# A hybrid RG-LRU and attention trunk: new order of products, operand work and sums in the feed-forward units, and overlapped chains at their ends

## The chip, the core and the metric

The kernel runs on one core of a Trainium2 chip. The metric is the device time of one execution in microseconds. A core has these engines, each with a queue that it works off in order: TensorE (PE in the profile; PEld is its loading of stationary operands), VectorE (DVE), ScalarE (ACT), GpSimd (POOL) and SyncE (SP), which here only starts transfers. Semaphores order the work between engines. Matmuls read SBUF and write PSUM, of which there are eight banks of 512 float32 columns in each of 128 partitions.

## The reference

`x` is one sequence of 512 tokens with 1024 features, in float32. Layer 0 mixes tokens by an RG-LRU, layer 1 by stick-breaking attention with 16 heads; each is followed by a feed-forward block of 2816 hidden features, which the change is about.

```python
D_MODEL, SEQ, DEPTH, D_FF = 1024, 512, 2, 2816

def _rmsnorm(x, g):
    y = x * lax.rsqrt(jnp.mean(x * x, axis=-1, keepdims=True) + RMS_EPS)
    return y * g

def _swiglu(h, w_gate, w_up, w_down):
    g = h @ w_gate
    u = h @ w_up
    return (jax.nn.silu(g) * u) @ w_down

for i in range(DEPTH):
    x = x + mixer_i(_rmsnorm(x, norm_mix_g[i]))     # RG-LRU, then attention
    x = x + _swiglu(_rmsnorm(x, norm_ffn_g[i]), ffn_w_gate[i], ffn_w_up[i], ffn_w_down[i])
return _rmsnorm(x, final_g)
```

## The kernel before

Every float32 factor is split into a high and a low part, and a product is the sum of three matmuls (`mm3`): high by high, high by low, low by high. So each chunk of weights, 128 x 1024 float32, has to be loaded and split before use: ScalarE casts `wh` (L294), and VectorE, or for a few chunks POOL, subtracts to get `wl` (L295).

The feed-forward block uses a Strassen-like scheme with seven products in place of eight, written g1 to g7 for the gate and up matrices and d1 to d7 for the down matrix. Some products take sums of weight blocks. For gate and up, these sums are mostly made by DMA: POOL starts transfers that add a block to a buffer in SBUF (`Piece.plus`, L87 to 90). The buffers are `bu` (g5, then g6, then g4, one after the other in the same place), `bv` (g3, g7) and `raw` (g1, g2). For the down matrix POOL makes them by four subtractions for each unit (`DownPiece.after`, L150 to 159, listed as L152). In units 0, 1 and 5 VectorE adds one sum directly (`direct`, L54 and L113).

The hidden features are worked in units 0 to 5 (`NU` = 5): 512 columns of weights in units 0 to 4, with two chunks a product, and 256 in unit 5, with one chunk. Unit u has its own g products and, from unit 1 on, the d products on the hidden features of unit u-1. Two more chunks ("last") follow. At the end of the g products of a unit come silu and the gating; the result is turned by PE transposes (t0 and t1, L697) and made into the operands ha, hb and ht on ScalarE and VectorE (`operands`, L699 to 710). PSUM: two pairs of banks, A and B, for the g products; `db` and `tb` for the d products, with `tb` also for the turns.

The order is written by hand. In `ffn` all four compute engines keep program order, and there are two orders as strings: one for the chunks in `Unit` (L54 to 62), one for the steps in `ffn` (L841 to 848). `chunk()` (L317) takes the next chunk, splits chunks up to 4 ahead of it, and starts loads up to 9 ahead (`more`). What `soon` (L258) was given is issued when the next chunk is taken. `hold` (L247, L666) bounds how far the first unit is loaded while the stage before still runs.

Unit 0 has two steps of its own: the turn of the residual stream into y (x0 to x3, `turned`), and `stats` (L818), the norm's scale, which PE computes by summing `acc` (L465). Behind layer 0's block, PE multiplies the last two chunks, turns y back (`back`, L861) and makes the normalised input of attention (`norm_in`, L388), where V's products come first (L336 to 338). Behind layer 1's block `finish` (L476 to 494) adds the last products, does the final norm in four blocks of 128 tokens, one after the other, and stores.

Of the kernel before, what the change touches and what calls it, by code (L numbers as in the profile page):

```python
# [16 lines left out]
P = 128  # L17
S = 512
# [26 lines left out]
class Unit:  # L45
    def __init__(self, kern, l, u):
# [22 lines left out]
class Piece:  # L69
    LOADS = {1: ("raw", 0), 2: ("raw", 2), 5: ("bu", 0), 3: ("bv", 3)}  # L70
    HOME = {1: 1, 2: 2, 5: 5, 6: 5, 4: 5, 3: 3, 7: 3}
    NEXT = {5: 3, 6: 2, 3: 1}
    last = {}

    def __init__(self, unit, q, c):
        self.unit, self.q, self.c = unit, q, c
        self.pool = (q, c) in ((7, 1), (2, 1)) and unit.u > 0 and unit.np == 2

# [13 lines left out]
    def ready(self):  # L92
        old = self.last.get((self.unit.kern, self.c))
        return self.q != 5 or old is None or old.u == self.unit.u or (old, 4, self.c) in self.unit.kern.done

    def load(self):
# [6 lines left out]
        if q == 5:  # L103
            self.plus(1)
            self.last[kern, self.c] = un
# [4 lines left out]
    def sums(self):  # L110
        un, kern = self.unit, self.unit.kern
        if self.q == 6 and un.direct:
# [17 lines left out]
class DownPiece(Piece):  # L130
    def __init__(self, unit, q):
        self.unit, self.q, self.c = unit, q, 0
        self.pool = q in (5, 4)

    def ready(self):
        return True

    def load(self):
        un, kern = self.unit, self.unit.kern
        for k in {1: ("11",), 2: ("21",), 6: ("12", "22")}.get(self.q, ()):  # L140
            t = un.d[k] = kern.raw_buf() if self.q < 6 else self.buf("d" + k, kern.fp, 1)
            kern.nc.sync.dma_start(t, un.down[("11", "21", "12", "22").index(k)])

    def source(self):
        return self.unit.d[{1: "11", 2: "21", 6: "t", 5: "11", 7: "12", 3: "22", 4: "t"}[self.q]]

    def sums(self):
        pass

    def after(self):  # L150
        kern, d = self.unit.kern, self.unit.d
        sub = lambda o, x, y: kern.soon(lambda: kern.nc.gpsimd.tensor_tensor(d[o], d[x], d[y], ALU.subtract))  # L152
        if self.q == 1:
            d["t"] = self.buf("dt", kern.fp, 1)
            sub("11", "12", "11")
            sub("t", "22", "11")
            sub("12", "22", "12")
        elif self.q == 6:
            sub("t", "21", "t")


class Kern:
    def __init__(self, ctx, tc, a, out):
# [15 lines left out]
        self.later, self.done = deque(), set()  # L179
# [40 lines left out]
    def plan(self):  # L220
# [26 lines left out]
        self.hold = next(i for i, e in enumerate(full) if isinstance(e, Piece)) + 6  # L247
# [10 lines left out]
    def soon(self, f):  # L258
        self.later.append((self.used, f))
# [57 lines left out]
    def chunk(self, ahead=None):  # L317
# [3 lines left out]
        while self.later and self.later[0][0] <= i:  # L321
# [954 lines left out]
```

## Time and profile before

| what | us |
|---|---|
| three executions | 1199.16, 1203.34, 1203.98 (median 1203.34) |
| the profiled execution | 1200.12, its span 1198.4 |
| RG-LRU layer | from 0 to 167.6 |
| feed-forward block 0 | from 167.6 to about 545 |
| attention | from about 545 to 815.8 |
| feed-forward block 1 | from 815.8 to 1198.4 |
| TensorE busy | 1118.7 |

In the views a row of the timeline gives the start, the busy time, the engine, the line, the operation, output and inputs, and in brackets the idle time before it and what ended it. A row of the waits gives the engine and line that waited, behind the arrow the engine and line waited for, and the total, the number and the longest of these waits in microseconds. DVE, ACT and POOL do not count as busy while they wait.

### The profile page before, as it was taken

To read this page: it belongs to the slowest core of one execution; us is meant where nothing else is said; L and a number is where in the kernel's file an instruction comes from. 1 tells how busy PE (TensorE), PEld (TensorE's weight loads), DVE (VectorE), ACT (ScalarE), POOL (GpSimd) and SP (SyncE) were. 2 spreads that over 40 slices of the span, in tenths; PEclk is the share of its full clock that TensorE was granted. 3 is DMA by queue.
4 is the path that set the end of the run, shared out by engine and by line. 5 is a ranking of instruction groups with operands and counts; after the bars stand their busy time and mean duration, and the time that the engine had idled before them with its cause. 6 is when DMAs were issued, how large, how long until landed. Compare 5 with 4: busy or idle time off the path is not lost. (4 is left out here: it accounts for less than half of the span.)

```text
span 1198.4 us, 14804 instructions
## 1 busy us (share of the span) xinstructions
PE 1118.7 (93%) x5265; PEld 917.2 (77%) x5265; DVE 921.5 (77%) x1243; ACT 703.2 (59%) x1076; POOL 416.9 (35%) x268
## 2 busy tenths in 40 slices
PE   9999998899999999899999999899889999999895
PEld 6887786678787877777888888677668878787784
DVE  6978885766888878875478898777577778778786
ACT  6697574556454553534489999766463545454453
POOL 2541221243536363413044444311134444434430
PEclk9999998999999999999999999999899999999998
DMA  7522326557585846332244334122737667675421
GB/s 273 150 88 88 112 101 165 115 159 178 145 204 134 218 112 187 106 92 71 82 125 102 93 89 118 41 89 106 177 69 210 142 185 166 167 174 134 107 53 70
DMA packets 47529, 155.68 MB, mean 130 GB/s; under 512 B 5856, under 2 KB 6880, under 8 KB 47456
## 3 DMA queue, kind: packets, MB, share of 16 engines
q1 hardware_dynamic: 36224, 113.84, 28.5%
q0 software_dynamic: 11232, 40.90, 19.5%
q8 instruction: 41, 0.67, 0.2%
q14 instruction: 32, 0.26, 0.1%
HBM read 144.23 MB, written 2.10 MB: 122 GB/s over the span
## 5 line engine op out<-in xcount | busy, mean ns | idle before, releaser
L691 PE MATMUL bank<-wl,ow 128*128 128x512 f32 (+1 forms) x480 | 182.0, 379 | 19.0 <-DVE wl L295 19.0
L690 PE MATMUL bank<-wh,ow 128*128 128x512 f32 (+1 forms) x480 | 182.7, 381 | 3.0 <-ACT r L769 2.5
L294 ACT CAST wh<-raw 128x1024 fp32r<-128x1024 f32 (+1 forms) x144 | 145.3, 1012 | 66.2 <-PE bank L692 27.5
L692 PE MATMUL bank<-wh,ow 128*128 128x512 f32 (+1 forms) x480 | 181.3, 378 | 0.6 <-DVE ow L401 0.6
L295 DVE TENSOR_TENSOR wl<-raw,wh 128x1024 fp32r<-128x1024 f32 (+1 forms) x100 | 131.9, 1321 | 64.8 <-ACT wh L294 63.4
L295 POOL TENSOR_TENSOR wl<-raw,wh 128x1024 fp32r<-128x1024 f32 (+1 forms) x44 | 108.6, 2468 | 143.5 <-ACT wh L294 143.5
L90 POOL DMA_DIRECT2D bu<-w_gu x56 | 49.2, 883 | 298.8 <-DVE wl L295 223.8
L691 PEld LDWEIGHTS bank<-wl,ow 128*128 128x128 f32 x480 | 92.4, 192 | 38.7 <-DVE wl L295 23.1
L294 ACT CAST wh<-bu 128x1024 fp32r<-128x1024 f32 x66 | 69.5, 1053 | 82.7 <-PE bank L692 38.1
L295 DVE TENSOR_TENSOR wl<-bu,wh 128x1024 fp32r<-128x1024 f32 x66 | 85.4, 1294 | 31.5 <-ACT wh L294 30.4
L690 PEld LDWEIGHTS bank<-wh,ow 128*128 128x128 f32 x480 | 92.2, 192 | 21.2 <-ACT r L769 3.6
L692 PEld LDWEIGHTS bank<-wh,ow 128*128 128x128 f32 x480 | 92.2, 192 | 16.8 <-DVE ow L401 1.0
L336 PE MATMUL bank<-uh,wh 128*128 128x512 f32 x256 | 102.6, 402 | 1.3 <-ACT uh L392 0.7
L338 PE MATMUL bank<-uh,wl 128*128 128x512 f32 x256 | 100.4, 393 | 1.1 <-DVE wl L295 1.0
L337 PE MATMUL bank<-ul,wh 128*128 128x512 f32 x256 | 100.1, 391 | 0.3 <-DVE ul L393 0.3
L682 DVE TENSOR_TENSOR y<-y,bank 128x512 f32<-128x512 f32 x140 | 89.9, 678 | 11.0 <-PE bank L692 10.7
L294 ACT CAST wh<-bv 128x1024 fp32r<-128x1024 f32 x44 | 45.4, 1050 | 87.6 <-DMA bv<-w_gu 84.7
L295 DVE TENSOR_TENSOR wl<-bv,wh 128x1024 fp32r<-128x1024 f32 x36 | 44.0, 1240 | 45.3 <-ACT wh L294 45.1
L1026 POOL TENSOR_TENSOR spl<-t,sph 128x512 fp32r<-128x512 f32 (+1 forms) x32 | 36.3, 1158 | 85.5 <-DVE sph L1025 79.8
L691 PE MATMUL bank<-wl,hth 128*128 128x512 f32 x160 | 62.4, 390 | 0.2 <-POOL wl L295 0.2
L447 POOL TENSOR_TENSOR acc<-acc,t 128x512 f32<-128x512 f32 x20 | 27.7, 1383 | 100.1 <-ACT t L445 93.1
L690 PE MATMUL bank<-wh,hth 128*128 128x512 f32 x160 | 62.5, 390 | 0.0
(249 smaller groups left out, 2947.8 us busy)
## 6 DMA issues: line engine op xcount, KB each, us to landing
bu<-w_gu POOLq DMA_DIRECT2D x56, 512.0 KB, 6.9
raw<-w_gu SPq DMA_DIRECT2D x44, 512.0 KB, 3.6
raw<-w_dn SPq DMA_DIRECT2D x24, 512.0 KB, 3.9
bv<-w_gu SPq DMA_DIRECT2D x22, 512.0 KB, 4.0
bu<-w_gu SPq DMA_DIRECT2D x22, 512.0 KB, 4.7
bv<-w_gu POOLq DMA_DIRECT2D x22, 512.0 KB, 7.0
d<-w_dn SPq DMA_DIRECT2D x20, 512.0 KB, 4.8
raw<-w_qk SPq DMA_DIRECT2D x16, 512.0 KB, 3.5
```

What stands on the lines that cost most here:

```text
L90: kern.soon(lambda: kern.nc.gpsimd.dma_start(t, self.part(n), accum_op=ALU.add))
L294: self.nc.scalar.copy(wh[:, c], raw[:, c])
L295: self.wl_engine(i).tensor_tensor(wl[:, c], raw[:, c], wh[:, c].bitcast(F32), ALU.subtract)
L336: mm(out, lhsT=wh, rhs=xh, start=first, stop=False)
L337: mm(out, lhsT=wh, rhs=xl, start=False, stop=False)
L338: mm(out, lhsT=wl, rhs=xh, start=False, stop=last)
L447: self.acci = eng.tensor_tensor(self.acc, self.acc, sq, ALU.add)
L682: add = lambda o, a, b: nc.vector.tensor_tensor(o, a, b, ALU.add)
L690: mm(out, lhsT=xh, rhs=wh, start=first, stop=False, skip_group_check=True)
L691: mm(out, lhsT=xh, rhs=wl, start=False, stop=False, skip_group_check=True)
L692: mm(out, lhsT=xl, rhs=wh, start=False, stop=last, skip_group_check=True)
L1026: nc.gpsimd.tensor_tensor(sl[:, w], sp[:, w], sh[:, w].bitcast(F32), ALU.subtract)
```

## The change

It does the following:

- The order of the g products starts with g5 in every unit, and g3 comes before d1. Unit 0 gives g4 and g2 banks of their own (`tb`, `db`), and g3 adds into B. Its copies of u2 and the statistics now stand where the list below shows.
- Both turns of a unit are one step, `tt`, after g1, into `tb` and `db`; `operands(0)` stands ahead of g6 and `operands(1)` (`o1`) behind it. In `operands` the split of ha comes first.
- The direct sums of VectorE are left to unit 5; units 0 and 1 get accumulating DMAs for them.
- The down sums: d11 and d12, d22 are loaded together for d1. POOL now makes dt = d22 - d12 and d12 = d12 - d11 at that load, put off by one chunk, and d12 = d21 - d11 after d5. VectorE makes d11 = dt + d11 for d6. `later` is a list with due numbers; loads run 11 ahead, `hold` is 8 instead of 6.
- In unit 5 the last turn `tn` writes into the ht slots (`hn`), before d4 and d3.
- At the end of block 0 five last products come first, then `back` of half the features with adds and norm in pieces between the other last products, and V's first chunk (`v_chunk`) ahead of the second `back`.
- `finish` works block by block in an overlapped way: POOL multiplies by g, ScalarE scales three and a half of the four blocks, and fewer small steps are left on VectorE.

```diff
-        self.direct = u in (0, 1, NU)
+        self.direct = u == NU
         if u == 0:
-            order = "g1 g3 g5 g2 g6 g7 g4"
-        elif u == 1:
-            order = "g1 g5 g6 d1 g3 d2 d6 g7 d5 d7 g4 d3 d4 g2"
+            order = "g5 g1 g6 g3 g4 g7 g2"
         elif u < NU:
-            order = "g5 g1 g6 d1 g3 d2 d6 g7 d5 d7 g4 d3 d4 g2"
+            order = "g5 g1 g6 g3 d1 d2 g7 d6 d5 d7 g4 d3 d4 g2"
         else:
-            order = "g5 g1 g6 d1 g3 d2 d6 d5 g7 d7 g4 g2 d4 d3"
+            order = "g5 g1 g6 g3 d1 d2 d6 g7 d5 g4 g2 d7 d4 d3"
...
-        for k in {1: ("11",), 2: ("21",), 6: ("12", "22")}.get(self.q, ()):
-            t = un.d[k] = kern.raw_buf() if self.q < 6 else self.buf("d" + k, kern.fp, 1)
+        for k in {1: ("12", "22", "11"), 2: ("21",)}.get(self.q, ()):
+            t = un.d[k] = kern.raw_buf() if k in ("11", "21") else self.buf("d" + k, kern.fp, 1)
             kern.nc.sync.dma_start(t, un.down[("11", "21", "12", "22").index(k)])
+        if self.q == 1:
+            un.d["t"] = self.buf("dt", kern.fp, 1)
+            self.minus("t", "22", "12", 1)
+            self.minus("12", "12", "11", 1)
...
     def sums(self):
-        pass
+        kern, d = self.unit.kern, self.unit.d
+        if self.q == 6 and not self.summed:
+            self.summed = True
+            kern.nc.vector.tensor_tensor(d["11"], d["t"], d["11"], ALU.add)
 
     def after(self):
-        kern, d = self.unit.kern, self.unit.d
-        sub = lambda o, x, y: kern.soon(lambda: kern.nc.gpsimd.tensor_tensor(d[o], d[x], d[y], ALU.subtract))
-        if self.q == 1:
-            d["t"] = self.buf("dt", kern.fp, 1)
-            sub("11", "12", "11")
-            sub("t", "22", "11")
-            sub("12", "22", "12")
-        elif self.q == 6:
-            sub("t", "21", "t")
+        if self.q == 5:
+            self.minus("12", "21", "11")
...
-        more = 9 if ffn else self.AHEAD_LOAD
+        more = 11 if ffn else self.AHEAD_LOAD
...
+        for t in range(NT):
+            gather(t, 0)
+            if t == NT - 1:
+                store(t - 1)
+            gather(t, 1)
+            if 0 < t < NT - 1:
+                store(t - 1)
+        store(NT - 1)
...
                 if u == 0:
-                    order = "g1 x0 g3 x1 g5 g2 g6 stats g7 gate1 x2 g4 x3"
-                elif u == 1:
-                    order = "g1 t0 g5 t1 g6 d1 g3 d2 d6 g7 d5 d7 g4 d3 d4 g2"
+                    order = "g5 x0 g1 x1 g6 stats g3 x2 g4 x3 g7 g2"
                 elif u < NU:
-                    order = "g5 t0 g1 t1 g6 d1 g3 d2 d6 g7 d5 d7 g4 d3 d4 g2"
+                    order = "g5 g1 tt g6 o1 g3 d1 d2 g7 d6 d5 d7 g4 d3 d4 g2"
                 else:
-                    order = "g5 t0 g1 t1 g6 d1 g3 d2 d6 d5 g7 d7 g4 g2 d4 tn d3"
+                    order = "g5 g1 tt g6 o1 g3 d1 d2 d6 g7 d5 g4 g2 d7 tn d4 d3"
...
-                for n in range(8):
+                for n in range(5):
+                    more(n)
+                back(0)
+                take(0)
+                gain(0)
+                more(5)
+                more(6)
+                take(1)
+                more(7)
+                gain(1)
+                take(2, 3)
+                self.v_chunk(self.bank[4:], 0)
+                gain(2, 3)
+                back(1)
+                for m in range(4, KT):
+                    take(m)
+                    gain(m)
```

The following lists give instructions in the order in which they stand in an engine's queue: line, operation, output and inputs, and shape. Numbers in the names tell buffers apart.

ScalarE around the statistics of unit 0 in the first block, before (`u20` and `u21` are the copies of u2 from pair A; `st` is the root for the scale; the casts read a `bu` or `bv` chunk):

```order
L294 CAST wh37_1631<-bu_161_1382 128x1024
L294 CAST wh38_1651<-bv_158_1376 128x1024
L294 CAST wh39_1669<-bv_159_1378 128x1024
L294 CAST wh440_1685<-bu_160_1380 128x1024
L793 COPY u20_1499<-bank0_70 128x512
L793 COPY u21_1500<-bank1_71 128x512
L452 ACT_TABLE_LOAD
L452 ACTIVATE st_131<-bank6_76,eps_126 128x4
```

And now:

```order
L296 CAST wh34_1579<-bv_180_1510 128x1024
L807 COPY r10_1493<-bank0_70 128x512
L807 COPY r11_1494<-bank1_71 128x512
L296 CAST wh35_1598<-bv_181_1512 128x1024
L296 CAST wh436_1615<-bu_136_1268 128x1024
L829 COPY u20_1495<-bank0_70 128x512
L829 COPY u21_1496<-bank1_71 128x512
L458 ACT_TABLE_LOAD
L458 ACTIVATE st_131<-bank6_76,eps_126 128x4
```

The two casts of bv directly ahead of the copies were those for g7, for which bv has had a block added by DMA; now the casts of bv there are those for g3, of bv as loaded, and one of bu for g4.

TensorE at the beginning of the first block, second chunk of the first g product; `a11` and `ow` are operands made of the block's input x, the ones with the highest numbers of its last part, m=7. Before:

```order
L690 MATMUL bank0_70<-wh29_1517,a11_127_1213 128x512
L691 MATMUL bank0_70<-wl29_1518,a11_127_1213 128x512
L692 MATMUL bank0_70<-wh29_1517,a11_127_1213 128x512
L690 MATMUL bank0_70<-wh29_1517,a11_133_1257 128x512
L691 MATMUL bank0_70<-wl29_1518,a11_133_1257 128x512
```

And now:

```order
L727 MATMUL bank2_72<-wh29_1514,ow_163_1417 128x512
L728 MATMUL bank2_72<-wl29_1515,ow_163_1417 128x512
L729 MATMUL bank2_72<-wh29_1514,ow_164_1418 128x512
L727 MATMUL bank2_72<-wh29_1514,ow_174_1471 128x512
L728 MATMUL bank2_72<-wl29_1515,ow_174_1471 128x512
L729 MATMUL bank2_72<-wh29_1514,ow_175_1472 128x512
```

The first product was g1 with `a11`, which is made of the first half of x alone; it is g5 now, with the high part `ow_174_1471` and the low part `ow_175_1472` of m=7. VectorE makes this low part here:

```order
L434 SCALAR_TENSOR_TENSOR t173_1466<-t171_1464,t172_1465 128x256
L297 TENSOR_TENSOR wl31_1523<-raw169_1436,wh31_1522 128x1024
L297 TENSOR_TENSOR wl432_1540<-bu_136_1268,wh432_1539 128x1024
L407 TENSOR_TENSOR ow_175_1472<-t172_1465,ow_174_1471 128x512
L407 TENSOR_TENSOR ow_178_1475<-t173_1466,ow_178_1475 128x256
```

Two splits of weights stand ahead of it.

POOL between unit 4 and unit 5 of the first block. `wl123` is the low part for d4 of unit 4 and `wl125` that for the second chunk of its g2; `bu_268` is unit 5's. Before:

```order
L295 TENSOR_TENSOR wl123_3512<-dt_262_3263,wh123_3511 128x1024
L295 TENSOR_TENSOR wl125_3554<-raw267_3438,wh125_3553 128x1024
L90 DMA bu_268_3456<-w_gu 128x1024
L152 TENSOR_TENSOR raw270_3515<-d12_275_3577,raw270_3515 128x1024
L152 TENSOR_TENSOR dt_277_3639<-d22_276_3579,raw270_3515 128x1024
L152 TENSOR_TENSOR d12_275_3577<-d22_276_3579,d12_275_3577 128x1024
```

And now:

```order
L297 TENSOR_TENSOR wl123_3523<-d12_255_3125,wh123_3522 128x1024
L138 TENSOR_TENSOR dt_274_3507<-d22_272_3503,d12_271_3501 128x1024
L138 TENSOR_TENSOR d12_271_3501<-d12_271_3501,raw273_3505 128x1024
L297 TENSOR_TENSOR wl125_3565<-raw267_3403,wh125_3564 128x1024
L86 DMA bu_268_3458<-w_gu 128x1024
```

Unit 5's subtractions moved from behind `wl125` to ahead of it, and `d12_255`, which `wl123` reads, lies in the same place as `d12_271`, the next unit's. The same place between two units of two chunks (here 1 and 2) reads, before the change, with `bu_205` and `bu_206` the two chunks of the next unit's g5:

```order
L90 DMA bu_205_2085<-w_gu 128x1024
L90 DMA bu_206_2106<-w_gu 128x1024
L90 DMA bu_205_2085<-w_gu 128x1024
L90 DMA bu_206_2106<-w_gu 128x1024
L152 TENSOR_TENSOR raw211_2205<-d12_215_2287,raw211_2205 128x1024
```

And now:

```order
L297 TENSOR_TENSOR wl62_2188<-raw204_2032,wh62_2187 128x1024
L86 DMA bu_205_2087<-w_gu 128x1024
L138 TENSOR_TENSOR dt_216_2217<-d22_214_2213,d12_213_2211 128x1024
L138 TENSOR_TENSOR d12_213_2211<-d12_213_2211,raw215_2215 128x1024
L86 DMA bu_206_2108<-w_gu 128x1024
L86 DMA bu_205_2087<-w_gu 128x1024
```

There two subtractions now stand between the first accumulating DMA of chunk 0 and that of chunk 1.

More of the change, by code (lines that the diff above doesn't have):

```diff
@@ L104, in load @@
             self.plus(1)
[L105 removed]
+            kern.chain[self.c] = un
     def source(self):
@@ L246, in plan @@
         self.wq = {}
-        self.hold = next(i for i, e in enumerate(full) if isinstance(e, Piece)) + 6
+        self.hold = next(i for i, e in enumerate(full) if isinstance(e, Piece)) + 8
         self.loaded = self.split = self.used = 0
@@ L331, in chunk @@
                 pass
+        if ffn and self.split < n and isinstance(self.chunks[self.split], Piece):
+            self.chunks[self.split].sums()
         return self.wq.pop(i)
@@ L496, in rglru, with v_chunk @@
+    def v_chunk(self, pv, c):
+        wh, wl = self.chunk()
+        for kk in range(2):
+            k = 2 * c + kk
+            cs = ts(kk, S)
+            for t in range(NT):
+                uh, ul = self.u[k]
+                self.mm3(pv[t], uh[:, ts(t)], ul[:, ts(t)], wh[:, cs], wl[:, cs], k == 0, k == KT - 1)
     def rglru(self):
@@ L697, in turn, with operands @@
                         nc.tensor.transpose(b[:, ts(t)], (u2 + b5)[t][:, ts(f)], self.ident)
-            def operands(p):
-                bx, by = tb
+            def operands(p, banks):
+                bx, by = banks
                 cx, ta, tc_ = (self.tmp() for _ in range(3))
                 nc.scalar.copy(cx, bx)
+                split([t[:, p] for t in ha], cx[:, T0])
                 add(ta[:, T0], cx[:, T1], by[:, T1])
@@ L707, in operands @@
                 split([t[:, p] for t in hb], by)
-                split([t[:, p] for t in ha], cx[:, T0])
                 for i, t in enumerate((ta, tc_)):
@@ L807, in g7 @@
                         add(b5[j][:, :w], b5[j][:, :w], A[j][:, :w])
+                    if u == 0:
+                        for j in range(2):
+                            add(sg[j][:, :w], sg[j][:, :w], A[j][:, :w])
+                        gate2()
                 def g4():
-                    product(4, A, False)
-                    sg = [self.tmp() for _ in range(2)]
-                    for j in range(2):
-                        self.last = nc.scalar.activation(sg[j][:, :w], A[j][:, :w], AF.Silu, scale=rs(2 + j))
-                    for j in range(2):
-                        nc.vector.scalar_tensor_tensor(b5[j][:, :w], b5[j][:, :w], nrs(2 + j), sg[j][:, :w],
-                                                       ALU.mult, ALU.mult)
+                    product(4, B4, u == 0)
+                    sg[:] = [self.tmp() for _ in range(2)]
+                    if u == 0:
+                        for j in range(2):
+                            nc.scalar.copy(sg[j][:, :w], B4[j][:, :w])
+                    else:
+                        gate2()
                 def stats():
```

159 lines of the change are left out of this document (88 added, 71 removed).

## The prediction

> **What bounds the kernel now.** I read the page's busy shares first, then the waits of TensorE stage by stage, then the timelines around the longest of them.
>
> ```profile
> PE 1118.7 (93%) x5265; PEld 917.2 (77%) x5265; DVE 921.5 (77%) x1243; ACT 703.2 (59%) x1076; POOL 416.9 (35%) x268
> ```
>
> TensorE (PE) is busy for 93% of a span of 1198.4 us. The change keeps its 5266 instructions, so only two things can become shorter: the 80 us in which PE is idle, and the stretches at half clock that follow idle time. The next two fences give PE's waits in the two feed-forward stages, each row with total, times and longest; first 167 to 553 us, then 815 to 1185 us.
>
> ```profile
> PE bank L691 <- DVE wl L295: 9.8, 5, 2.4
> PE bank L690 <- ACT u L793: 4.7, 1, 4.7
> PE bank L690 <- ACT hah L686: 3.8, 2, 1.9
> PE bank L697 <- DVE u L782: 2.4, 2, 2.1
> PE bank L338 <- DVE ul L393: 2.4, 2, 1.3
> PE bank L697 <- DVE hbl L681: 2.1, 2, 1.7
> PE bank L690 <- DVE y L682: 1.4, 1, 1.4
> PE bank L690 <- ACT r L769: 1.2, 1, 1.2
> PE bank L465 <- DVE r L682: 0.9, 1, 0.9
> PE bank L336 <- ACT uh L392: 0.9, 3, 0.5
> PE bank L692 <- DVE ow L401: 0.6, 1, 0.6
> ```
>
> ```profile
> PE bank L691 <- DVE wl L295: 9.2, 4, 2.4
> PE bank L690 <- ACT u L793: 3.4, 1, 3.4
> PE bank L465 <- DVE r L682: 2.3, 1, 2.3
> PE bank L690 <- DVE x L1131: 2.3, 1, 2.3
> PE bank L690 <- ACT hah L686: 2.2, 2, 1.8
> PE bank L697 <- DVE hbl L681: 1.7, 1, 1.7
> PE bank L690 <- ACT r L769: 1.3, 2, 1.2
> ```
>
> Those rows add up to 30.2 and 22.4 us. No resource is full there: each wait is one operand that comes late on an engine that has time to spare. Half clock comes on top, in eight windows of the two stages (from 198.2, 246.0, 549.7, 819.4, 853.5, 897.9, 1024.2 and 1136.8 us). The first and the last, in a view that gives length, busy time of PE, weight loads, DVE, ACT and POOL, and then the granted clock:
>
> ```profile
> 198.20:208.40 10.20, 5.96 (x14) 4.71 (x15) 6.70 (x13) 5.84 (x8) 0.03 (x1) 0.50 0.46 151
> 1136.80:1140.20 3.40, 3.40 (x19) 3.40 (x18) 3.37 (x7) 0.18 (x1) 0.71 (x1) 0.51 0.02 5
> ```
>
> In 3.40 us at half clock PE does 1.70 us of full-clock work: such a window costs **1.7 us**. The 10.2 us window has 5.96 us of work in it and costs 3.0.
>
> A rule of the Trainium skill bears on this: "TensorE: Matmul & The Clock Gate", Part 1, says that the clock halves after about 3.4 us of idling. The last window here followed waits of 1.7 and 1.2 us (hbl and r in the second list), so the measurement decides: shorter waits can lead to it too. By the page's rule the waits of 2.4 us and less would not be what brought six of the windows, their 10 us would stay, and the sum below would give about 1176.
>
> **The change, part by part** (plus saves, minus costs; against the profiled execution, 1200.1 us with a span of 1198.4).
>
> *Statistics of unit 0.* L690 <- ACT u (4.7 and 3.4) is ScalarE's queue: the copies of u2 stand behind casts of bv, which wait for an accumulating DMA.
>
> ```profile
> 199.91 1.04 ACT L294 CAST wh<-bv 128x1024 fp32r<-128x1024 f32 x1 [5.15 <-DMA bv<-w_gu]
> 201.80 1.07 ACT L793 COPY u<-bank 128x512 f32<-128x512 f32 x2
> ```
>
> In the new order the casts ahead of the copies read a plainly loaded bv, and g3 follows the statistics on the other pair of banks. Both waits go, with L465's: 0.9 + 4.7 + 3.0 (half clock) = **+8.6** in the first stage. In the second, 2.3 + 3.4 + 2.3 (half clock, by the same halving) less 0.5 for x2's turn, directly ahead of g4 in the same banks: **+7.5**.
>
> *Start of the unit.* g5 now comes first, and it needs ow of m=7, which is made last. The rows behind its two operands:
>
> ```profile
> 173.27 0.92 ACT L406 CAST ow<-t 128x512 fp32r<-128x512 f32 x2
> 174.29 1.22 DVE L295 TENSOR_TENSOR wl<-bu,wh 128x1024 fp32r<-128x1024 f32 x1
> 175.42 2.13 DVE L401 TENSOR_TENSOR ow<-t,ow 128x512 fp32r<-128x512 f32 x2
> 167.57 0.39 PE L690 MATMUL bank<-wh,a 128*128 128x512 f32 x1
> ```
>
> PE starts a matmul every 0.227 us (2.72 us for the twelve of a product). From 167.57, g5's fifteen without m=7 end at 170.97. The first of the two casts ends at about 173.9: 2.9 idle. Two matmuls later the low part is wanted; its subtraction stands third behind two wl splits on VectorE, as before, and is through at about 177.2: 2.9 more. 5.8 less the 0.6 of before, with one window: **-6.9**. In the second stage the same wait takes the place of 2.3 and has a window already: 3.7 + 0.3 = **-4.0**. Bounds of each: -9, if both idle times bring their own window, and -3, if the scheduler's earlier rows let ScalarE and VectorE run ahead.
>
> *Unit 1.* Both turns stand together after g1, and operands(0) and (1) have g6 and g3 beside them. Of the lists above, wl 2.4 and 0.8, hah 1.9, hbl 0.4 and two of 0.3 and 0.4 are unit 1's in the first stage, 6.2 in all; wl 2.4, hah 1.8 and one of 0.4 in the second, 4.7; each stage has one window there: **+7.7** and **+6.2**, keeping back 0.2.
>
> *Units 2 to 4.* In each, the wl for g3 is late by 2.2 or 2.3 (six of the nine waits in the two L691 rows). The reason is on two engines:
>
> ```profile
> 280.09 0.88 POOL L90 DMA_DIRECT2D bu<-w_gu  x1 [1.66 <-DMA bu<-w_gu]
> 298.64 2.43 POOL L152 TENSOR_TENSOR raw<-d,raw 128x1024 f32<-128x1024 f32 x1
> 301.14 2.49 POOL L152 TENSOR_TENSOR dt<-d,raw 128x1024 f32<-128x1024 f32 x1
> 302.47 0.69 DVE L681 TENSOR_TENSOR hbl<-bank,hbh 128x512 fp32r<-128x512 f32 x1 [0.65 <-ACT hbh L686]
> 303.84 3.50 DVE L681 TENSOR_TENSOR htl<-t,hth 128x512 fp32r<-128x512 f32 x2
> ```
>
> With GpSimd (POOL) in its subtractions, two htl take 3.50 us; the like hbl, with one input in PSUM, takes 0.69. The two subtractions that are left move to the tail of the unit before, and there they stand between the accumulating DMAs of the two chunks of g5. Behind the first (280.09) they take 0.88 + 2.43 + 2.49, so the second goes out at 286 to 288 and lands 6.9 us later by the row below: at 295 at the latest. g6's second chunk needs it at about 300, after a cast of 1.05 and a split of 1.2 or so (the rows of 199.91 and 174.29). I keep 0.7 a unit for the thin margin (bounds 0 and 2.2): 3 x (2.2 - 0.7) = **+4.5**; second stage (7.0 with a short one of POOL's, a window) 7.0 + 1.7 - 2.1 = **+6.5**.
>
> ```profile
> bu<-w_gu POOLq DMA_DIRECT2D x56, 512.0 KB, 6.9
> d<-w_dn SPq DMA_DIRECT2D x20, 512.0 KB, 4.8
> ```
>
> *Unit 4 to unit 5.* Unit 5 has one chunk a product, so its subtractions are issued earlier in program order: two stand between wl of d4 and wl of g2's second chunk.
>
> ```profile
> 457.27 2.75 POOL L295 TENSOR_TENSOR wl<-dt,wh 128x1024 fp32r<-128x1024 f32 x1
> 461.02 2.40 POOL L295 TENSOR_TENSOR wl<-raw,wh 128x1024 fp32r<-128x1024 f32 x1 [1.01 <-ACT wh L294]
> 464.50 0.39 PE L690 MATMUL bank<-wh,ow 128*128 128x512 f32 x1
> ```
>
> Before, that wl was ready at 463.4, and PE wanted it at 464.50 + 2.72 + 0.23 = 467.45. Now SyncE's load of d12 waits for wl of d4, which reads the same buffer: 460.0 + 4.8 (landing) + 2.43 + 2.49 + 2.40 = 472.1. The new wait is 4.7, with a window **-6.4**, in each stage (bounds 0, if wl of d4 comes 4.7 earlier because one subtraction ahead of it went; -8 with a second window). Queued behind the waiting subtraction on POOL are also the accumulates for unit 5, which has a few us of slack left by this stop itself.
>
> *Unit 5.* Its waits (u 2.4, hbl 1.7, r 1.2, hah 1.9, y 1.4 in the first stage, 8.5 before rounding; hbl 1.7, r 1.2, hah and u 0.7 in the second, 3.6 and a window) are broken by d2, d6 and g7 between producer and user. I keep back 1: **+7.5**, **+4.3**.
>
> *To attention.* L338 and L336 wait 3.3 us, with a window. Five last turns, then back and norm in pieces, with V's first chunk as cover, leave 0.5: **+4.5**.
>
> *What else is added.* VectorE gains one sum of 1024 columns in each unit with a down part, and units 0 and 1 lose two each; at 1.22 apiece (the 174.29 row) the ten new ones are 12 us on an engine with 277 us idle. The one for d6 stands ahead of d6's split, with g3, d1 and d2 running (four products, 10.9 us): nothing, bounds 0 and 1.2 a unit. The same for four more accumulating DMAs and the longer look-ahead, which only let loads start earlier.
>
> *The end.* After the last matmul, finish runs four row blocks one after another, each like this:
>
> ```profile
> 1189.02 1.41 DVE L493 SCALAR_TENSOR_TENSOR y<-y,st,raw 128x512 f32<-128x512 f32 x2
> 1194.03 1.41 DVE L493 SCALAR_TENSOR_TENSOR y<-y,st,raw 128x512 f32<-128x512 f32 x2
> 1183.73 0.39 PE L692 MATMUL bank<-wh,hbl 128*128 128x512 f32 x1
> ```
>
> A block costs 5.0 us (1194.03 - 1189.02), and from PE's end at 1184.1 to the last product at 1195.4 it is 11.3. In the new order the blocks overlap. The last one still takes its own 5.0, and ScalarE, in order, has the block before it in front: two squares and two scaled copies of 512 columns, some 0.65 each (0.53 in the pair of 201.80, 0.69 on VectorE at 302.47), 2.6. That is 7.6: **+3.7** (bounds 2, if the block chains of 5.0 stay half apart, and 6.3, if nothing is in front).
>
> First stage: -6.9 + 8.6 + 7.7 + 4.5 - 6.4 + 7.5 + 4.5 = 19.5. Second: -4.0 + 7.5 + 6.2 + 6.5 - 6.4 + 4.3 + 3.7 = 17.8. Together **37.3**: span 1161.1, profiled execution 1162.8. The median before, 1203.3, is 3.2 above its profiled execution, so the like median is **1166**.
>
> **The rivals.**
> *New waits covered:* the start and unit 4's end show nothing, because ScalarE and VectorE come earlier in the new order and wl of d4 too. For it: both engines are idle 23% or more of the span. Against it: the rows above have dated ends. It gives back 6.9 + 4.0 + 2 x 6.4 = 23.7: **1142**.
>
> *The stall moves but stays:* POOL's two subtractions now meet VectorE's splits for the next g5 and g1, whose inputs both lie in SBUF, as htl's do. If one held split reaches PE in each of the eight units 1 to 4, at the 2.2 of before where I put 0.2 to 0.7, it is about 6 x 1.5 + 2 x 2.0 = 13, with three windows 18: **1184**. This is the reading of the Trainium skill, "SBUF — State Buffer", on the two separate sides: the port pair that both engines share is held for a whole instruction by whichever began, and a VectorE operation with two SBUF inputs waits. The 3.50 beside 0.69 agrees.
>
> *Slower:* POOL's queue order decides. Suppose that the held-back second accumulate of g5 lands so late that g6's second chunk waits 5.5 us for it in every one of those eight units, with a window: 8 x (5.5 + 1.7 - 0.6) = 53, of which 5 are windows already in the sum: 1166 + 48 = **1214**. Slower than before it becomes from 4.2 us a unit on (8 x 5.3 - 5 = 37). For that the DMA would have to land at about 302 instead of 295, and its 6.9 us be 14: the rows have nothing like it.
>
> *The change doesn't do what it says* would be the statistics' wait surviving: 16 us stay, 1182, inside the range and counted with the moved stall.
>
> **How the numbers follow.** Forecast 0.56, covered 0.15, moved stall 0.23, slower 0.06. The unknown costs taken at their far ends (start 2.1 and 5.0 more in the two stages, unit 4's end 1.7 each, units 2 to 4 9.0, the end 1.7) add up to 21, and with a quarter of VectorE's sums (3) they give 1190; at their near ends they give the first rival's time and somewhat less. **Range 1142 to 1190.** A measurement of this kernel can tell about 0.5% from no change: 1197 to 1209. Faster 0.91, same 0.04, slower 0.05.
>
> **What would show it.** Right: no L793-like wait at the statistics; PE idle twice for about 2.9 us near 171 and 174; one wait of 4 to 5 us on POOL's wl just before unit 5, in both stages; no wl wait of 2.2 at g3. Wrong: PE waiting on a wl or a DMA at g6's second chunk in units 1 to 4, or DVE splits of 2.9 us and more beside POOL's subtractions at the units' ends; a tail after the last matmul of more than 12 us.

## The result, and the profile after

| | before | changed |
|---|---|---|
| median of 4 runs, us | 1202.21 | 1188.30 |
| lowest and highest | 1199.16, 1203.98 | 1184.85, 1190.24 |
| span of the profiled execution | 1198.4 | 1188.5 |

The ratio is 0.9884, with a 95% interval from 0.9852 to 0.9916. The change makes the kernel 1.2% faster, by 14 us in the medians and by 9.9 us in the profiled executions, where 37 were forecast. The time lies in the forecast range, near its upper end; the gain is less than half of the one that was forecast.

The first row of the page says that TensorE's share went up by one point only:

```profile
PE 1115.6 (94%) x5265; PEld 913.9 (77%) x5265; DVE 945.1 (80%) x1235; ACT 710.6 (60%) x1087; POOL 425.0 (36%) x273
```

VectorE is busy for 24 us more, with fewer instructions; an operation that is held up after its start counts as busy until it ends (see the gatings below). The largest of TensorE's waits in the two feed-forward blocks of the changed kernel (total, times, longest), from 166 to 538 us and then from 808 to 1175 us:

```profile
PE bank L728 <- POOL wl L297: 9.5, 2, 8.9
PE bank L727 <- DVE y L719: 3.1, 5, 0.7
PE bank L727 <- ACT ow L412: 2.8, 1, 2.8
PE bank L729 <- DVE ow L407: 2.6, 1, 2.6
PE bank L728 <- DVE wl L297: 2.1, 6, 0.6
PE bank L727 <- DVE t L718: 1.6, 1, 1.6
PE bank L727 <- ACT r L807: 1.1, 1, 1.1
PE bank L727 <- ACT b L802: 0.8, 1, 0.8
```

```profile
PE bank L728 <- POOL wl L297: 6.7, 1, 6.7
PE bank L727 <- DVE y L719: 3.3, 6, 0.6
PE bank L727 <- ACT ow L412: 3.2, 1, 3.2
PE bank L729 <- DVE ow L407: 2.5, 1, 2.5
PE bank L728 <- DVE wl L297: 1.9, 7, 0.6
PE bank L727 <- DVE t L718: 1.6, 1, 1.6
PE bank L727 <- DVE r L719: 1.4, 2, 1.0
PE bank L727 <- ACT b L802: 0.8, 1, 0.8
```

The statistics' waits of 4.7 and 3.4 us are gone, and so are the nine waits on VectorE's wl of up to 2.4. In their place stand the two forecast stops (ow at the start; POOL's wl, larger than forecast) and, spread over units 1 to 5, short waits of 0.2 to 1.6 us for wl, y, r, t and b, in more places than the prediction had. Stage by stage, from the start of the first matmul of each unit in TensorE's timeline (us, minus is shorter; "stop" is the wait on POOL's wl before unit 5 with its half-clock loss; unit 0 of the second block counts from where attention ends, so that the wait for x before the change is in it):

| stage | forecast | first block | forecast | second block |
|---|---|---|---|---|
| unit 0, start and statistics | -1.7 | -1.3 | -3.5 | -2.8 |
| unit 1 | -7.7 | -8.4 | -6.2 | -4.2 |
| units 2 to 4 without the stop | -4.5 | +1.8 | -6.5 | -2.8 |
| the stop | +6.4 | +11.3 | +6.4 | +9.5 |
| unit 5 | -7.5 | -3.3 | -4.3 | -1.2 |
| to attention, or last products and finish | -4.5 | -6.5 | -3.7 | -0.9 |

The two columns of results and 0.95 us of the unchanged first layer add up to the 9.9 us, but for rounding. Of the 27 that are missing, 10.0 are in units 2 to 4, 8.0 in the stop, 7.3 in unit 5 and 2.8 in the end.

### The profile page after: what moved, and what is told of

It reads as the page before. It is cut to its first block, busy times and chain, and to the rows that moved or that the text cites. A ratio compares the mean times of both kernels' runs of the same rounds, so it can differ in the third digit from the quotient of the medians.

```text
span 1188.5 us, 14810 instructions
## 1 busy us (share of the span) xinstructions
PE 1115.6 (94%) x5265; PEld 913.9 (77%) x5265; DVE 945.1 (80%) x1235; ACT 710.6 (60%) x1087; POOL 425.0 (36%) x273
## 5 line engine op out<-in xcount | busy, mean ns | idle before, releaser
L297 DVE TENSOR_TENSOR wl<-raw,wh 128x1024 fp32r<-128x1024 f32 (+1 forms) x110 | 155.6, 1416 | 50.0 <-ACT wh L296 46.7
L86 POOL DMA_DIRECT2D bu<-w_gu x64 | 56.0, 875 | 225.9 <-DVE wl L297 121.5
L297 DVE TENSOR_TENSOR wl<-bu,wh 128x1024 fp32r<-128x1024 f32 x66 | 101.9, 1546 | 31.4 <-ACT wh L296 31.1
L297 POOL TENSOR_TENSOR wl<-raw,wh 128x1024 fp32r<-128x1024 f32 (+1 forms) x34 | 81.3, 2390 | 113.2 <-ACT wh L296 113.2
L727 PE MATMUL bank<-wh,hth 128*128 128x512 f32 x192 | 75.6, 394 | 5.4 <-DVE y L719 5.4
L297 POOL TENSOR_TENSOR wl<-d,wh 128x1024 fp32r<-128x1024 f32 x20 | 53.6, 2682 | 63.6 <-DVE u L719 32.9
L728 PE MATMUL bank<-wl,hth 128*128 128x512 f32 x192 | 74.8, 390 | 0.0
L729 PE MATMUL bank<-wh,htl 128*128 128x512 f32 x192 | 74.8, 390 | 0.0
```

The costliest lines, as they stand in the source:

```text
L86: kern.soon(lambda: kern.nc.gpsimd.dma_start(t, self.part(n), accum_op=ALU.add))
L297: self.wl_engine(i).tensor_tensor(wl[:, c], raw[:, c], wh[:, c].bitcast(F32), ALU.subtract)
L727: mm(out, lhsT=xh, rhs=wh, start=first, stop=False, skip_group_check=True)
L728: mm(out, lhsT=xh, rhs=wl, start=False, stop=False, skip_group_check=True)
L729: mm(out, lhsT=xl, rhs=wh, start=False, stop=last, skip_group_check=True)
```

## The experiments

All start from the changed kernel unless said otherwise. "Ratio" is against the kernel before, run on the same chip; the changed kernel has 0.9884. Spans are those of the profiled executions (1188.5 for the changed kernel). They and the lengths of single units carry most readings, since several ratios have intervals that touch that of the changed kernel. Two profiled executions can differ by 5 us in units that have the same code (see e7), so a unit's length is compared with more than one kernel where the difference is small. The kernel before had medians of 1197.75 to 1199.58 us beside these runs and 1202.21 in the result, so medians of different groups are not compared directly.

### The stop between units 4 and 5: e1, e8, e11

GpSimd's timeline there in the changed kernel, and TensorE's matmul behind it:

```profile
450.08 2.72 POOL L297 TENSOR_TENSOR wl<-d,wh 128x1024 fp32r<-128x1024 f32 x1
459.37 2.50 POOL L138 TENSOR_TENSOR dt<-d,d 128x1024 f32<-128x1024 f32 x1 [6.57 <-DMA d<-w_dn]
461.94 3.20 POOL L138 TENSOR_TENSOR d<-d,raw 128x1024 f32<-128x1024 f32 x1
465.11 2.33 POOL L297 TENSOR_TENSOR wl<-raw,wh 128x1024 fp32r<-128x1024 f32 x1
467.50 0.80 PE L728 MATMUL bank<-wl,ow 128*128 128x512 f32 x1 [8.89 <-POOL wl L297]
```

The queue is the one that the prediction drew: the wl that TensorE waits for stands behind two subtractions, which wait for a load of d, which waited for the first wl.

```diff
-            self.minus("t", "22", "12", 1)
-            self.minus("12", "12", "11", 1)
+            self.minus("t", "22", "12", 1 + 2 * (self.unit.u == NU))
+            self.minus("12", "12", "11", 1 + 2 * (self.unit.u == NU))
```

This is e1; e11 has a 7 in place of the 2.

> Theory (POOL's queue order): in both blocks the two subtractions of unit 5 stand ahead of the low part for g2's second chunk of unit 4, and that low part waits with them. With the order of these three turned round, TensorE's two waits for it (8.89 and 6.69 us) and the half-clock windows behind them (about 2.3 and 2.8 us) go: 19 to 21 us less than the changed kernel, about 1168. Rival (the wait is only passed on, to unit 5, because its sums come later): the two waits go and others of 5 us or more stand in unit 5: less than 10 us gained.

1177.32 us, ratio 0.9824 [0.9809, 0.9839], span 1175.9. Both waits on POOL's wl are gone, so the queue's order made them. But new ones of 4.12 and 2.10 us stand at g1 of unit 5, on VectorE's r: a part of the rival, with waits below its 5 us. Units 4 and 5 together got shorter by 9 us in the two blocks, not by 20. VectorE and GpSimd at that place in e1:

```profile
459.66 3.42 DVE L110 TENSOR_TENSOR bu<-bu,bv 128x1024 f32<-128x1024 f32 x1
```

```profile
458.73 3.26 POOL L138 TENSOR_TENSOR d<-d,raw 128x1024 f32<-128x1024 f32 x1
```

The direct sum, 1.22 us by itself, takes 3.42 here. It ends 1.09 us after GpSimd's subtraction is through, and r waits behind it. e8 took these sums from VectorE (with e1's edit, and the gating of e5):

```diff
-        self.direct = u == NU
+        self.direct = False
```

> The kernel of e1 (subtractions of unit 5 behind the low part of g2) with, in addition, the gating of b5 out of PSUM and unit 5's direct sum made by DMA, so that VectorE has none of the two-SBUF-input operations that took 5.5 and 3.4 us there. Theory (GpSimd's subtractions and splits hold VectorE up between units 4 and 5): the waits of 4.12 and 2.10 us that e1 shows at g1 of unit 5 fall below 1 us, and with their half-clock window 6 to 9 us go against e1. Rival (these waits are TensorE's bank being read late for another reason): they stay above 2 us in the first block.

1182.79 us, ratio 0.9860 [0.9825, 0.9895], span 1182.7. The theory of this run fell: the waits at g1 grew to 7.39 and 7.22 us. ScalarE's cast, which VectorE's wl and then r wait for, shows why:

```profile
463.01 1.04 ACT L296 CAST wh<-bu 128x1024 fp32r<-128x1024 f32 x1 [11.51 <-DMA bu<-w_gu]
```

The sum is now an accumulating transfer, and GpSimd issues it behind the same two subtractions.

> The changed kernel with unit 5's two subtractions put off by seven chunks more, so that on GpSimd they stand behind the low part of g2 and behind both transfers for g4 and g7 of unit 5. Theory (GpSimd's subtractions first held the low part of g2 back, and in e1 VectorE's direct sum): TensorE's waits of 8.89 and 6.69 us are gone, and those of 4.12 and 2.10 us that e1 had at g1 of unit 5 fall below 1 us; 15 to 21 us less than the changed kernel, in the profiles. Rival (VectorE is late there even without the subtractions): a wait above 2 us stays at g1 of unit 5, or comes at d6, whose sum needs them.

1176.72 us, ratio 0.9824 [0.9795, 0.9854], span 1175.5. With the subtractions put off further, the wait at g1 is 1.37 us in the first block and under 0.3 in the second, but 4.63 us stand at g3 of unit 5 in each, for ScalarE's copies of b5. GpSimd and VectorE in e11:

```profile
469.56 2.72 POOL L138 TENSOR_TENSOR dt<-d,d 128x1024 f32<-128x1024 f32 x1
```

```profile
469.85 2.72 DVE L718 TENSOR_TENSOR hal<-t,hah 128x256 fp32r<-128x256 f32 x1
472.50 0.41 DVE L719 TENSOR_TENSOR t<-t,bank 128x256 f32<-128x256 f32 x1
```

In each of the three places where the two subtractions were put, a VectorE operation of that moment with two inputs in SBUF is held up: here hal, 2.72 us, where the next one, with an input in PSUM, takes 0.41. Of the stop's 20.8 us, units 4 and 5 of e11 bring back 13.

### The start: e2

```diff
-            order = "g5 g1 g6 g3 g4 g7 g2"
+            order = "g1 g5 g6 g3 g4 g7 g2"
...
-                    order = "g5 x0 g1 x1 g6 stats g3 x2 g4 x3 g7 g2"
+                    order = "g1 x0 g5 x1 g6 stats g3 x2 g4 x3 g7 g2"
```

> Theory (operands of the last eighth of x have a fixed date): with g1 ahead of g5 in unit 0, TensorE has 5.4 us of work more before it needs them, and its two waits at the start of each block (2.80 + 2.56 and 3.24 + 2.52 us) fall below 1 us, and in the first block the half-clock window goes with them: 9 to 13 us less than the changed kernel. Rival (the order of g5's accumulating transfers comes with it): g6 or the statistics of unit 0 wait 3 us or more in their place, and less than 5 us is gained.

1180.30 us, ratio 0.9846 [0.9824, 0.9869], span 1178.8. The waits for ow are gone, but in the second block TensorE waits 2.25 us for x at the start, as it did before the change. Unit 0 is 7.3 us shorter in the first block and, with that wait, 4.9 in the second. The statistics do not wait. In the first block 3.51 us, with a half-clock window, come back at g5 of unit 1 on VectorE's wl, so that unit 1 is 5.0 longer. The theory holds; a part is given back later, not at the place that the rival named.

### The gatings: e5 and e12

In the changed kernel and before, silu writes to SBUF, and VectorE multiplies b5 by it, both in SBUF. This is the edit in e12; e5 has the same in units 1 to 5 of the changed kernel.

```diff
-                    sg = [self.tmp() for _ in range(2)]
...
-                        self.last = nc.scalar.activation(sg[j][:, :w], A[j][:, :w], AF.Silu, scale=rs(2 + j))
+                        self.last = nc.scalar.activation(A[j][:, :w], A[j][:, :w], AF.Silu, scale=rs(2 + j))
...
-                        nc.vector.scalar_tensor_tensor(b5[j][:, :w], b5[j][:, :w], nrs(2 + j), sg[j][:, :w],
+                        nc.vector.scalar_tensor_tensor(b5[j][:, :w], b5[j][:, :w], nrs(2 + j), A[j][:, :w],
```

> The changed kernel, with the silu of g4 left in its PSUM bank, so that VectorE's gating of b5 has one input in PSUM instead of two in SBUF; nothing else moves. Theory (VectorE and GpSimd exclude each other where VectorE reads two SBUF inputs): the gatings that took 1.6 to 3.3 us beside GpSimd's work in the changed kernel (0.75 by themselves) take 0.8 us or less everywhere. Rival (they are slow because of semaphores or transfers): they stay at 1.6 us or more in units 1 to 4. For the time of the kernel both expect little, 0 to 3 us less, as this gating is not what TensorE waits for.

1181.33 us, ratio 0.9854 [0.9813, 0.9895], span 1179.4.

> The kernel before, with the gating of b5 out of PSUM as in e5. Theory (it was the change that brought GpSimd's subtractions beside the gatings): before the change they stood elsewhere, so there is nothing to gain, within 2 us of the kernel before. Rival (the gatings were held up before, too, and e5 mended an old cost): 5 us or more less, as in e5.

1197.48 us, ratio 0.9994 [0.9973, 1.0016]. The rows of the groups, with count, busy time and mean in ns, for htl and the gating, from the kernel before, the changed kernel, e5 and e12 in turn:

```profile
L681 DVE TENSOR_TENSOR htl<-t,hth 128x512 fp32r<-128x512 f32 x40 | 47.7, 1233 | 0.0
L815 DVE SCALAR_TENSOR_TENSOR b<-b,nrs,t 128x512 f32<-128x512 f32 (+1 forms) x24 | 26.9, 1149 | 1.3 <-ACT t L813 1.1
```

```profile
L847 DVE SCALAR_TENSOR_TENSOR b<-b,nrs,t 128x512 f32<-128x512 f32 (+1 forms) x24 | 51.1, 2162 | 4.2 <-ACT t L844 4.2
L718 DVE TENSOR_TENSOR htl<-t,hth 128x512 fp32r<-128x512 f32 x40 | 25.7, 683 | 0.0
```

```profile
L718 DVE TENSOR_TENSOR htl<-t,hth 128x512 fp32r<-128x512 f32 x40 | 25.7, 683 | 0.0
L847 DVE SCALAR_TENSOR_TENSOR b<-b,nrs,bank 128x512 f32<-128x512 f32 (+1 forms) x20 | 13.5, 689 | 6.5 <-ACT bank L845 6.5
```

```profile
L681 DVE TENSOR_TENSOR htl<-t,hth 128x512 fp32r<-128x512 f32 x40 | 47.7, 1232 | 0.0
L814 DVE SCALAR_TENSOR_TENSOR b<-b,nrs,bank 128x512 f32<-128x512 f32 (+1 forms) x24 | 15.9, 692 | 1.1 <-ACT bank L812 1.1
```

A part of the gain of units 2 to 4 went here. Before, GpSimd held up htl, 1233 ns in the mean; with the change htl is free (683) and the gatings are held up for longer (1149 to 2162). What VectorE gains in the one, 22.0 us, it pays in the other, 24.2. With an input in PSUM the gating takes 689 ns. Units 2 to 4 of both blocks, without the wait on POOL's wl, take 376.5 us in the changed kernel, 375.4 and 373.6 in e3 and e7, which have the same units, and 368.7 in e5: 5 to 8 us less. e8 against e1, the other pair with and without this edit, has 363.9 against 369.7. That is half or more of the 10.0 that were missing. The expectation had the mechanism right and the effect on the time too small: it took the gating to be off TensorE's path. How the path runs can be seen between units 3 and 4 of the first block of the changed kernel, on VectorE, GpSimd and TensorE:

```profile
387.22 6.18 DVE L847 SCALAR_TENSOR_TENSOR b<-b,nrs,t 128x512 f32<-128x512 f32 x2
396.95 3.54 DVE L297 TENSOR_TENSOR wl<-bu,wh 128x1024 fp32r<-128x1024 f32 x1
400.41 3.40 DVE L297 TENSOR_TENSOR wl<-raw,wh 128x1024 fp32r<-128x1024 f32 x1
403.74 1.27 DVE L719 TENSOR_TENSOR r<-r,bank 128x512 f32<-128x512 f32 x2
```

```profile
387.11 2.73 POOL L297 TENSOR_TENSOR wl<-d,wh 128x1024 fp32r<-128x1024 f32 x1
389.53 2.65 POOL L297 TENSOR_TENSOR wl<-raw,wh 128x1024 fp32r<-128x1024 f32 x1
396.70 2.70 POOL L138 TENSOR_TENSOR dt<-d,d 128x1024 f32<-128x1024 f32 x1
399.48 3.26 POOL L138 TENSOR_TENSOR d<-d,raw 128x1024 f32<-128x1024 f32 x1
```

```profile
404.56 0.47 PE L727 MATMUL bank<-wh,a 128*128 128x512 f32 x1 [0.57 <-DVE r L719]
```

The gatings are held up beside GpSimd's splits for d4 and g2. Behind them in VectorE's queue, the splits for the next g5 and g1 are held up beside the two subtractions that the change moved here; r comes after them, and g1 waits for it. Eleven such splits, of 3.4 to 3.8 us each, stand around the ends of units 1 to 3 in the two blocks. The products g5 and g1 of units 2 to 4 are 6.4 us longer in all than without a wait, and 1.1 us in e5, although splits are held up there too (3.62 and 3.41 us ahead of unit 3 of the first block). Nothing is gained by the same edit before the change (e12), although it cuts the gatings by 11 us there too: there htl keeps its 47.7 us, and TensorE's waits of 2.2 us are those for the wl behind it.

### The distance of d6 and d7: e6 and e10

```diff
-            order = "g5 g1 g6 g3 d1 d2 g7 d6 d5 d7 g4 d3 d4 g2"
+            order = "g5 g1 g6 g3 d1 d2 g7 d6 d5 g4 d7 d3 d4 g2"
```

The same in the list of steps.

> The changed kernel with g4 between d5 and d7 in units 1 to 4 instead of behind d7. Theory (bank distance): d7 adds into the banks that d6 has just filled, with one product between, and waits 0.57 to 0.61 us in each of the eight units for VectorE's adds on y; with g4 between, this wait goes, but d4 then follows d7 with one product between, so that it comes back there in part: 0 to 5 us less, and the eight waits named y L719 ahead of d7 are gone. Rival (VectorE is simply late at that time, wherever the product stands): waits of the same size stand at the next use of a freed bank.

1191.35 us, ratio 0.9945 [0.9914, 0.9976], span 1188.2. The waits of 0.6 us for y ahead of d7, which stood in seven of the eight units, are gone, so the distance made them. But in two units d4 now waits 3.4 us for y.

> e9 with g4 between d5 and d7 as in e6. Theory (e6's new waits of 3.4 us came from gatings that GpSimd held up, in front of the adds on y): with the gatings out of PSUM these waits do not come back, and the eight waits of 0.6 us ahead of d7 stay away: 3 to 7 us less than e9. Rival (d4 is now too close to d7): as many waits of 0.6 us or more ahead of d4 or d3, and no gain.

1170.81 us, ratio 0.9769 [0.9733, 0.9805], span 1171.1, 17 us more than e9. The waits of 3.3 to 3.6 us at d4 stand in four units, though the gatings are out of the way: the theory fell. In each of the six units of e6 and e10 with such a wait, a split on VectorE stands ahead of the adds on y and takes 6.3 to 6.6 us beside two splits of GpSimd; in the other ten no VectorE operation of that stretch takes more than 3.5. In unit 2 of the first block of e10, VectorE first, then GpSimd:

```profile
320.76 6.56 DVE L297 TENSOR_TENSOR wl<-raw,wh 128x1024 fp32r<-128x1024 f32 x1 [0.22 <-ACT wh L296]
```

```profile
321.22 2.72 POOL L297 TENSOR_TENSOR wl<-d,wh 128x1024 fp32r<-128x1024 f32 x1
323.58 2.66 POOL L297 TENSOR_TENSOR wl<-raw,wh 128x1024 fp32r<-128x1024 f32 x1
```

So GpSimd holds VectorE up again, at another operation. That d4 feels it because it is close behind d7, as the rival said, fits, but no run separates the two.

### The end: e3 and e7

e3 moves the one small VectorE operation that waits for the squares (L495) to the roots, and puts store(t-1) behind both adds of block t.

> Theory (VectorE's queue): in finish one small VectorE operation, which waits for ScalarE's sum of squares, stands ahead of the next add, so the blocks stay some 3.4 us apart. With it moved behind the adds, the tail after TensorE's last matmul falls from 13.5 us to 9 to 11. Rival (ScalarE's own queue of squares and scaled copies is the bound): the tail stays within 1 us of 13.5.

1186.22 us, ratio 0.9904 [0.9881, 0.9926], span 1188.4. From TensorE's last matmul to the end it is 12.3 us instead of 13.5: nearer to the rival. The timelines of the changed kernel say more than the theory had taken from them, VectorE first, then ScalarE:

```profile
1181.02 0.67 DVE L492 TENSOR_TENSOR y<-y,bank 128x512 f32<-128x512 f32 x1
1183.17 0.21 DVE L502 TENSOR_SCALAR st<-st 128x1 f32<-128x1 f32 x1 [1.48 <-ACT t L493]
```

```profile
1181.19 1.33 ACT L509 ACTIVATE y<-y,st 128x512 f32<-128x512 f32 x2 [1.26 <-DVE st L505]
1182.43 0.61 ACT L493 ACTIVATE t<-y 128x512 f32<-128x512 f32 x1
```

The last add is made at 1181.0, six us after TensorE's last matmul. Its square stands behind two scaled copies of another block, which waited for VectorE, and VectorE then waits for the square: two in-order queues take turns. e7 takes this apart:

```diff
         for t in range(NT):
             gather(t, 0)
-            if t == NT - 1:
-                store(t - 1)
             gather(t, 1)
-            if 0 < t < NT - 1:
+            root(t)
+            if t:
                 store(t - 1)
         store(NT - 1)
```

Here root(t) is the small VectorE operation of e3 and the root behind it, without the scaling, and store gives one of its two scaled copies to VectorE.

> The changed kernel with finish as a pipeline: the root of a block is asked for behind its squares, its scaling comes one block later, and VectorE takes half of the scaled copies. Theory (both in-order queues, ScalarE's and VectorE's, wait for each other within each block): from TensorE's last matmul to the end of the span 8 to 10 us instead of 13.5, 3.5 to 5.5 us less in all. Rival (the last block's own chain is the bound): 12 us or more.

1181.73 us, ratio 0.9854 [0.9825, 0.9884], span 1178.8. The tail is 9.0 us, 4.5 less: the theory of this run holds. The other 5 us by which this span is shorter lie before the end, where this kernel has no edit.

### Unit 5: e13, e14, e17, e15

e13 puts the copies of b5 ahead of operands(0), in all units from 1 on; e14 puts g7 of unit 5 ahead of d1; e17 takes out the early call of sums at the end of chunk(), which brings VectorE's down sum (L157) behind operands(1).

> The changed kernel with the copies of b5 ahead of operands(0) in the step tt. Theory (ScalarE's queue): the wait of 0.83 us at g3 of unit 5 in each block, named ACT b, goes; 1 to 3 us less in all. Rival (the copies only change places with the operands): the wait for hah or hbl at d1 and d2 grows by as much, no gain.

1197.28 us, ratio 0.9978 [0.9954, 1.0002], slower than the changed kernel by its ratio.

> The changed kernel with g7 of unit 5 ahead of d1. Theory (in unit 5 a g product has one chunk and lasts 3 us, too short to hide operands(1)): with 3 us more of cover, the waits of 1.58 and 0.42 us at d1 fall below 0.5 us together in each block, 2 to 5 us less in all. Rival (g7's own chunk is not there yet): a wait of 1 us or more at g7, and no gain.

1193.65 us, ratio 0.9940 [0.9916, 0.9964].

> The changed kernel without the early call of sums, so that VectorE's sum for d6 stands behind operands(1) instead of ahead of it. Theory (the sum, 1.22 us, delays operands(1)): the wait of 1.58 us named DVE t at d1 of unit 5 falls to 0.4 or less in each block, and the waits of 0.6 us for wl at d2 in units 1 to 4 shrink; 2 to 6 us less in all. Rival (the sum is only moved, and d6 waits for it): a wait of about 1 us at d6, no gain.

1190.41 us, ratio 0.9914 [0.9879, 0.9950].

Each removes or halves the wait that it aims at, and each gets it back. In e13 the 0.83 at g3 goes, and the 1.58 at d1 becomes 3.38 in both blocks. In e14 the waits at d1 go, and 3.45 and 3.06 stand at g6 for ScalarE's r, which in the first block comes behind the cast of g7's own chunk, and that cast waited 7.18 for its transfer. In e17 the 1.58 becomes 0.78, and d6 waits 2.79 for y in both blocks; the waits for wl at d2 in units 1 to 4 stay as they were. Unit 5 took 48.8 and 47.4 us in the changed kernel; in the three it took 48.9 and 47.7, 51.0 and 51.1, 51.8 and 48.4. So the rivals hold in substance, and none of the three single causes is the one. e15, which joins e13 with e9, says the same:

> e9 with the copies of b5 ahead of operands(0). Theory (ScalarE's queue): e9's two longest waits, 3.85 and 3.26 us named ACT b in unit 5, fall below 1 us, 5 to 9 us less than e9 with the half-clock windows. Rival (VectorE, held up by GpSimd's subtractions there, is late with the operands as well): waits of 2 us or more for hah, hal or t at d1 instead.

1160.85 us, ratio 0.9646 [0.9599, 0.9693]: the waits for b5 are gone, and 5.12 and 5.37 us stand at d1 for VectorE's t. That is 7 us more than e9.

### Together: e4 and e9

e4 joins e1, e2 and e3.

> The three edits together. If the three costs are independent, the gains add: 30 to 37 us less than the changed kernel, 1151 to 1158. If one hides behind another, clearly less than the sum of the three runs alone.

1170.72 us, ratio 0.9767 [0.9750, 0.9784], span 1169.4: 19 us less than the changed kernel in the span, not 30 to 37, since the parts gave less than expected alone (12.6, 9.7 and 0.1 us in the spans).

> e11 with g1 ahead of g5 in unit 0 (e2), the pipelined finish (e7) and all gatings of b5 out of PSUM (e5, here in unit 0 too). If the four costs are independent: 15 to 20 (subtractions) + 8 to 10 (start) + 4 to 5 (finish) + 5 to 8 (gatings), 32 to 43 us less than the changed kernel, 1145 to 1156 us. If the gains overlap: above 1160.

**1153.77 us, ratio 0.9631 [0.9598, 0.9664], span 1153.0.** This beats both kernels, within the bounds expected for independent costs; its largest waits in the feed-forward blocks are the 3.85 and 3.26 us for b5 in unit 5 and 2.55 us at g5 of unit 1.

## Why the prediction was wrong

*What bounds the kernel:* right. The time followed TensorE's waits, and e9 shows that many of them can be removed.

*Statistics of unit 0, unit 1 of the first block, to attention:* right, within 2 us each; the waits that were named are gone. In unit 1 of the second block 2.0 of the 6.2 us are missing, with short waits of 0.4 to 0.6 us for r, hbl, wl and y.

*Start of the unit:* right in place and size: 2.80 and 2.56 us where 2.9 and 2.9 were worked out. e2 shows that it is the cost of putting g5 first.

*Unit 4 to unit 5:* the mechanism was right, the term was mis-sized, 6.4 against 11.3 and 9.5. From the end of d4's split to the end of g2's, the chain took 14.6 and 14.9 us in the two blocks where 12.1 were added up: GpSimd waited 6.57 and 5.05 us for the load of d and not 4.8, the second subtraction took 3.20 in both and not 2.49, and in the second block the first subtraction took 3.29 and the split 3.32. In the first block d4's split also ended only 2.7 us ahead of g2's first matmul, and not 4.5. The half clock covered 10 us and not 3.4. In the windows of half clock in the two blocks (length, then TensorE's busy time, ... , granted clock):

```profile
462.00:472.20 10.20, 4.71 (x11) 3.74 (x12) 1.64 (x2) 0.72 (x1) 6.25 (x3) 0.50 0.35 86
1107.10:1117.30 10.20, 5.62 (x15) 4.56 (x16) 5.63 (x4) 1.77 (x2) 5.41 (x3) 0.50 0.45 128
```

Half of the work in them, 2.4 and 2.8 us, is lost. That the clock falls during a wait this long is also what the Trainium skill says in "TensorE: Matmul & The Clock Gate", Part 1, and the trace agrees (waits of 8.89 and 6.69 us, granted clock 0.50).

*Units 2 to 4:* **this is the step that failed.** It said that the wait of 2.2 us was made by subtractions on GpSimd that block VectorE, which was right, and that moving two of them to the tail of the unit before would leave 0.7 a unit, for the sake of a DMA. That they and GpSimd's splits hold up VectorE in the tail as well was put at nothing. There VectorE has the gatings, and behind them the splits for the next g5 and g1, all with two inputs in SBUF, and r, for which g1 waits, comes last. Savings of 4.5 and 6.5 us were forecast; the first block lost 1.8 there and the second saved 2.8. The gatings are worth 5 to 8 of the 10.0 us between (e5); before the change there was nothing to gain from them (e12). To that come the waits of 0.6 us ahead of d7, from the new distance to d6, as e6 shows.

The splits of the next g5 and g1 are those that the prediction had named, but only in a rival. Their 3.4 to 3.8 us beside the subtractions are also a sign that it had set for being wrong (2.9 us and more); what they cost by themselves no run shows. The DMA was late in two units. In unit 2 of the first block ScalarE's cast for g6's second chunk waited 4.90 us for it, and behind that cast stood the copies of r1, for which g6's first matmul waited 1.13 us; in unit 1 of the second block these were 3.22 and 0.47.

The rule of "SBUF — State Buffer" in the Trainium skill, on the two separate sides, that a VectorE operation with two inputs in SBUF and a GpSimd operation that reads SBUF exclude each other for the whole instruction, should have been worked into the sum and not beside it. The runs bear it out: hal 2.72 us against 0.41, the gating 2162 ns against 689 with an input in PSUM.

*What else is added:* VectorE's new sum, put at 1.22 us, took 2.03 us in the mean; e17 shows that moving it gains nothing.

*Unit 5:* 3.3 and 1.2 where 7.5 and 4.3 were forecast. The statement that other products stand between producer and user was true of the order and not of the time. Moving the b5 copies, g7 or the down sum alone moves the waits and does not end them. What sets the length of unit 5 stays open.

*The end:* 10.0 us from TensorE's last matmul to the last product instead of 7.6. The step took only ScalarE's queue into account. e3 and e7 show that ScalarE and VectorE wait for each other.

*The rivals:* "new waits covered" did not happen; "slower" did not; "the stall moves but stays", at 1184, is nearest to what came, in the mechanism and in the time. That the time lies 1.7 us inside the range is owed to the far ends of its bounds and not to the sum.

## What to carry to other kernels

A subtraction on GpSimd is not free on VectorE: for every place to which it is moved, list the VectorE operations there that read two SBUF operands, and give them one in PSUM where a bank is at hand. When a wait is broken by a new order, price the next waits along the same queue, since several short ones can be worth the long one; and where a new order brings two uses of a bank nearer to each other, count the work between them. A chain that was timed in another place should be given a margin when it is moved: here each of the four links, a load, two subtractions and a split, took longer than its row in at least one block.

## What the runs showed of the hardware that was not expected

Waits add half-clock loss in a way that the length of the wait alone does not tell: the stop of 8.89 us and that of 6.69 us each came with 10.2 us of half clock, while the three waits of 0.8, 1.6 and 0.4 us in a row in unit 5 came with none. A VectorE operation can be held up by more than one GpSimd instruction: two in a row kept a gating of e1 for 5.49 us (VectorE's timeline, then GpSimd's).

```profile
447.92 5.49 DVE L847 SCALAR_TENSOR_TENSOR b<-b,nrs,t 128x512 f32<-128x512 f32 x1
```

```profile
447.75 2.74 POOL L297 TENSOR_TENSOR wl<-d,wh 128x1024 fp32r<-128x1024 f32 x1
450.23 2.61 POOL L297 TENSOR_TENSOR wl<-raw,wh 128x1024 fp32r<-128x1024 f32 x1
```

The gating began 0.17 us after the first split and ended 0.57 us after the second. The six splits of 6.3 to 6.6 us on VectorE in e6 and e10 also lie beside two GpSimd splits in a row.
